# A decoder block in split fp32: activation sums moved between unit pairs, w_down's fourth operand summed by DMA, and the first up units interleaved

## The chip, the cores and the metric

The kernel runs on one core of one Trainium2 chip. The metric is device time of one execution, in microseconds (us), the median over runs. TensorE (PE) multiplies, VectorE (DVE), ScalarE (ACT) and GpSimd (POOL) work on the operands, and SyncE (SP), POOL and ACT issue the DMAs. "PEld" is TensorE's loading of weights, which runs beside its matmuls.

## What is computed

One residual decoder layer on x of 512 positions by 1024 channels, all in float32. The change touches the second half, the channel sub-layer:

```python
h2 = rms_norm(x, norm2_g) * (1 + scale2) + shift2
u = causal_dwconv(h2 @ w_up, conv_w, conv_b)      # w_up: 1024 x 5632, window 3
u_g, u_v = jnp.split(u, 2, axis=-1)               # 2816 channels each
x = x + gate2 * ((jax.nn.silu(u_g) * u_v) @ w_down)
```

The vectors shift, scale and gate come from c through `ada_w`, 6 groups of 1024 columns; group 5 is gate2. The first half (attention with block selection, a pooling mixer, their gated sum and w_out) is not touched.

## The kernel before

**Split operands.** Every float32 operand of a matmul is split in two: a high half `hi` (ACT copies it to the fp32r type) and a low half `lo = raw - hi` (DVE). A product is then three matmuls: hi times hi, hi times lo, lo times hi (`mm3`, L127; `more`, L133, the same as a continuation of an open sum). `up_mm` (L1140) runs `mm3` over the 8 row blocks k of a unit, where a unit is 128 of w_up's columns. Matmuls take 512 positions, or 256 where only one half of the positions is ready or where the seven-product scheme works on halves.

**Order.** PE, DVE and ACT run in the order in which the program names the instructions; SP's and POOL's DMAs are placed by a planner at build time and issue as soon as what they wait for is done. Buffers are rings or pools of fixed size: `wraw` 5 raw weight units (128 x 1024), `whi` and `wlo` 4 each, `slots` 68 tiles of 128 x 512, 8 PSUM banks.

**First up units (L1328 to L1338).** When w_out's last products end, the first half of the positions is already normalized and transposed (`h2h`, `h2l`, by `take_h2(1, ...)`); the second half is still going through `o_norm` (L1042: the tiles `xn`). Units 0 to 3 start on positions 0 to 255. Unit 0 takes hi and lo weights times h2h for all k first and h2l after that (`up_late`, L1132). After unit 1 come the transposes of the second half (`turn_h2(3)`, PE line L919), `take_h2(3)`, which makes h2h and h2l of it block by block (ACT L932 and L934, DVE L935), and two ada sums; then units 2 and 3, and last all four units on positions 256 to 511. `ahead(name, n)` (L112) prepares the hi and lo halves (ACT L109, DVE L119) up to n units past the named one; up to six units are prepared this way.

**The up loop (L1423).** Pair j (0 to 21) is the gate unit and the value unit of 128 channels. Pairs in `SEVEN` (5, 6, 8, 9, 10, 12, 13, 14, 16 to 19) are computed with seven products of half size in place of eight (Strassen's scheme, Winograd's form; `seven`, L1291), 84 matmuls of 256 positions each; they need sums of the two weight units (`prep_seven`, L1248: steps s0 to s3, with halves named G, t1, R and V), made while the pair before is multiplied. R's second half is added in DVE line L1279. The other pairs are plain: 48 matmuls of 512 positions. In `seven`, `keep` (L1305) lets ACT copy a PSUM sum aside before the sum goes on; `ka` and `kb` are such copies.

**Behind the matmuls.** One pair late, `behind(0)` runs the convolution of pair j - 1 (`glu_a`; ACT L1124, four DVE steps L1128) and `behind(1)` its silu and product (`glu_b`; DVE L1158). Four pairs make one unit i of w_down's input (`fa["a11", i]` and so on; unit i has the pairs 4i to 4i + 3, and there are NU = 6 units, the last one half as wide). When the pair listed in `S_AT` has been through `behind(1)`, `s_sum` (L1164, DVE L1167) forms s1 = a21 - a22 of the unit with that place in the list, and the next `behind(0)` runs `s_split` (L1169): hi and lo of s1 and a11 (ACT L1176, DVE L1179) and the sums s2 and s3 (DVE L1181, L1182). `s_forms` is both at once. In a plain pair `behind(0)` comes after all preparation steps but the last, in a pair of seven products after the second (after the first where the next pair is plain).

**The down phases (L1515).** `w_down` is multiplied in seven products too, one after the other over all six units, 66 matmuls of 512 columns per phase (in the last one, two units are cut in halves). Here they are numbered 1 to 7: a11 b11, s1 t1, s2 t2, a12 b21, s3 t3, s4 b22, a22 t4. `d_ahead` keeps the splits of the weight operands (`d_split`; ACT L1391, DVE L1393) two units ahead. t1, t2 and t4 are running sums: the tile `ta` holds b11, and after its split an accumulating DMA from POOL's queue (L1396) adds b12, which makes t1, and after that b22, which makes t2. t4 is t2 + b21: `d_load` loads b21 again as a raw unit, and `d_add` (L1372, DVE L1378) adds `ta`. Around the matmuls of a unit the program places the splits of the activations for later phases (`split_s`, `split_a`; L214 and L215), the sum s4 (L1546), and the ada sums (`ada_col`: a load of 128 x 1024 into `wraw` and one DVE operation, L202). `finish` (L1476) combines the kept sums, multiplies by gate2, adds the residual and stores; it needs gate2 as rows, which `row_out` (L834, a small DMA of POOL) and `row_in` (ACT's queue) turn round.

Of the kernel before, what the change touches and what calls it, by code (L numbers as in the profile page):

```python
# [10 lines left out]
ALU = mybir.AluOpType  # L11
# [8 lines left out]
KT = D // P  # L20
# [14 lines left out]
PLAIN = 3  # L35
# [20 lines left out]
def block_kernel(tc, x, cvec, ada, wtok, wch, pool_w, wbr, wout, wup, wdn, pack, table, out):  # L56
# [4 lines left out]
    with ctx:  # L61
# [18 lines left out]
        def load_unit(src, name):  # L80
            raw = wraw_p.tile([P, src.shape[-1]], F32, tag="raw", name=f"raw_{name}")
            nc.sync.dma_start(raw, src)
            return raw
# [1045 lines left out]
                        t[:, n:], ps[:, : S - n], cw(i, 2 - n), t[:, n:], op0=ALU.mult, op1=ALU.add)  # L1129
            return res  # L1130

        def up_late(ps, w, c0, c1):  # L1132

            for k in range(KT):
                nc.tensor.matmul(ps[:, c0:c1], w[0][:, tslice(k)], h2h[k][:, c0:c1], start=k == 0, stop=False)
                nc.tensor.matmul(ps[:, c0:c1], w[1][:, tslice(k)], h2h[k][:, c0:c1], start=False, stop=False)
            for k in range(KT):
                nc.tensor.matmul(ps[:, c0:c1], w[0][:, tslice(k)], h2l[k][:, c0:c1], start=False, stop=k == KT - 1)

        def up_mm(ps, w, c0, c1):  # L1140
            for k in range(KT):
# [185 lines left out]

        first = []  # L1328
        for i in range(4):
            ahead(f"up{i}", min(2, 2 * PLAIN - 1 - i))  # L1330
            first.append((ready.pop(f"up{i}"), bank(f"u_{i}")))
            (up_mm if i else up_late)(first[i][1], first[i][0], 0, 256)
            if i == 1:
                take_h2(3, turn_h2(3))
                ada_col(5, 0)
                ada_col(5, 1)
        for w, ps in first:
            up_mm(ps, w, 256, 512)  # L1338
        pend, summed = [], []
        S_AT = [4, 7, 19, 20]  # L1340

        tsum = {("t3", i): dpool.tile([P, width(i)], F32, name=f"tsum_t3_{i}") for i in range(NU)}

# [14 lines left out]
        def d_load(m):  # L1358

            n, i = divmod(m, NU)  # L1360
            nm, w = FORMS[n], width(i)
            src = lambda b, c0=0, c1=w: wdn[plain[b], i][:, c0:c1]
            if nm == "b11":
                ta[i] = [slot(f"ta_{i}_{u}") for u in range(w // 512)]
                for u, t in enumerate(ta[i]):
                    nc.sync.dma_start(t, src("b11", u * 512, u * 512 + 512))
            elif nm[0] == "b" or nm == "t4":
                draw[m] = load_unit(src("b21" if nm == "t4" else nm), f"{nm}_{i}")
            elif nm == "t3":
                draw[m] = load_unit(tsum["t3", i], f"t3_{i}")  # L1370

        def d_add(m):  # L1372

            i = m - 6 * NU
            if 0 <= i < NU:
                for u, t in enumerate(ta.pop(i)):
                    r = draw[m][:, u * 512 : u * 512 + 512]
                    nc.vector.tensor_add(r, r, t)  # L1378

        def d_split(m):  # L1380

# [17 lines left out]
        def d_ahead(m):  # L1399

            m = min(m, len(FORMS) * NU - 1)
            while done[1] <= m:
                while done[0] <= min(done[1] + 2, len(FORMS) * NU - 1):
                    d_load(done[0])
                    done[0] += 1
                d_split(done[1])
                done[1] += 1
                d_add(done[1])

        def behind(n):  # L1410

# [11 lines left out]
        for j in range(NP):  # L1423
            if j + 1 == NP:
                steps = [lambda: d_ahead(0), lambda: d_ahead(1)]
            else:
                steps = [] if j < PLAIN else (prep_seven if j + 1 in SEVEN else prep_two)(j + 1)
            if j < 2:
                u = first[2 * j][1], first[2 * j + 1][1]
                behind(0)  # L1430
                if j == 1:
                    for st in prep_two(PLAIN):
                        st()
                behind(1)
                h_forms(j)
                ada_col(5, 2 + j)
            elif j in SEVEN:
                if len(steps) == 2:
                    mine = [steps[:1], [lambda: behind(0)], [lambda: behind(1)], steps[1:]]
                else:  # L1440
                    mine = [steps[:1], steps[1:2] + [lambda: behind(0)], steps[2:3] + [lambda: behind(1)], steps[3:]]
                u = seven(j, lambda n: [f() for f in mine[n]])
            else:
                if j < PLAIN:
                    for e in range(2):
                        upw[j, e] = ready.pop(f"up{2 * j + e}")
                u = [bank(f"u_{2 * j + e}") for e in range(2)]
                for st in steps[:-1]:
                    st()
                up_mm(u[0], upw.pop((j, 0)), 0, S)  # L1450
                behind(0)
                for st in steps[-1:]:
                    st()
                up_mm(u[1], upw.pop((j, 1)), 0, S)
                behind(1)
                if j in (2, 3):
                    h_forms(j)
            pend.append((j, *u))
            sum_load(j + 3)
            if j % 2 == 0:  # L1460
                t3_sum(j // 2)
        s_forms(NU - 2)
        behind(0)
        behind(1)

# [49 lines left out]
        for n, (an, bn, acc) in enumerate(phases):  # L1515
            last = n == len(phases) - 1
            held_ = []
            for i in range(NU):
                d_ahead(n * NU + i + (3 if n == i == 0 else 2))
                w = dready.pop(n * NU + i)  # L1520
                if due:
                    due.pop(0)()
                a = forms.pop((an, i))
                if last and i >= NU - 2:
                    held_.append((a, w, width(i) // 512))
                else:
                    for u in range(width(i) // 512):
                        for p in range(2):
                            step(acc, p, u, a, w, 0, 512, i == NU - 1 and u == width(i) // 512 - 1)
                if n == 0:  # L1530
                    if i == 2:
                        s_forms(NU - 1)
                    if i > 1:
                        split_s(i - 2)
                    if i == NU - 1:
                        ada_col(5, 4)
                elif n == 1:
                    if i in (0, 2, 4):
                        ada_col(5, 5 + i // 2)
                    if i < 2:  # L1540
                        split_s(NU - 2 + i)
                    forms["a12", i] = split_act(fa["a12", i], f"a12_{i}", width(i) // 2)
                elif n == 2:
                    split_a("s3", i)
                    s2 = fa.pop(("s2", i))
                    nc.vector.tensor_add(s2, s2, fa.pop(("a12", i)))  # L1546
                    fa["s4", i] = s2
                elif n == 3:
                    split_a("s4", i)
                    split_a("a22", i)  # L1550
                    if i == 2:
                        g2 = row_in(g2d, "g2", nc.scalar)
            if last:
# [6 lines left out]
                keep("s1", "X")  # L1560
            elif n == 1:
                keep("s5", "Y")
                g2d = row_out(5, "g2")
            elif n == 2:
                keep("s2", "X")
                fetch(0, 0)
# [78 lines left out]
```

## Time and profile before

| | |
|---|---|
| median of 3 runs | 669.06 us (667.11 to 671.19) |
| the profiled execution | 667.67 us, its span (first to last instruction) 665.9 us |
| mean granted TensorE clock | 0.997 |
| DMA | 140.21 MB, mean 211 GB/s |
| DMAs of `ta` from w_down, POOL's queue | 22 of 256 KB, median 8.8 us from issue to landing |
| loads of `raw_ada`, SP's queue | 48 of 512 KB, median 5.1 us |

Times in the views are counted from the first instruction. A row of the timeline gives start, length, engine, line, operation, written tile <- read tiles, shape, count, and in brackets how long the engine sat idle before it and what ended that. A row of the stretches gives the stretch, its length, then busy time and instructions of PE, PEld, DVE, ACT and POOL, the granted clock, the DMA engines' busy share and GB/s. A row of the waits gives the waiting instruction, what it waited for, the sum, the number of times and the longest. Matmul lengths overlap, since they are pipelined: how fast PE goes is read from starts or from a stretch and its count. PE's stretches used below are: first units 311.25 to 337.55, pairs 2 to 21 from there to 550.94, phase 1 from 550.94, phase 2 from 567.62, phase 4 from 597.54, phase 7 from 643.25.

### The profile page before, as it was taken

Reading aid. Unit: us, or ns where it says so; the run is one execution under the profiler, and the core shown is the slowest. Engines: PE = TensorE matmul, PEld = TensorE weight load, DVE = VectorE, ACT = ScalarE, POOL = GpSimd, SP = SyncE. Lnnn points to the kernel's source line nnn. Section 1 sums busy time; section 2 is a strip of 40 time slices with the busy share of each in tenths; the row PEclk is TensorE's granted clock in tenths of the full one; section 3 lists DMA queues with packets and bytes.
Section 4 is the critical chain, followed back from the end, with each engine's and each line's share of the span. In section 5 each row is a group of like instructions: output and inputs, shape, how many; then the busy total and the mean of one; then the engine's idle time right before and its main releaser. Section 6 shows DMA issues by size and latency. Waiting matters only on the chain.

```text
span 665.9 us, 10016 instructions
## 1 busy us (share of the span) xinstructions
PE 649.7 (98%) x3541; PEld 561.9 (84%) x3541; DVE 571.2 (86%) x990; ACT 394.6 (59%) x716; POOL 159.0 (24%) x203
## 2 busy tenths in 40 slices
PE   7999999999999999999999999899999999999996
PEld 5788788888888888888988999889999987878884
DVE  6997888898878878999699898978879989989776
ACT  7655346756665566576655666556657746768421
POOL 3003154433200046513411212121222023500000
PEclk9999999999999999999999999899999999999999
DMA  8887248999852686467877577584868485957841
GB/s 342 303 301 284 69 173 264 273 274 316 258 180 96 224 181 228 179 220 249 226 248 190 159 203 200 163 232 114 228 174 239 155 240 121 233 121 243 282 171 64
DMA packets 47657, 140.21 MB, mean 211 GB/s; under 512 B 6019, under 2 KB 6700, under 8 KB 47606
## 3 DMA queue, kind: packets, MB, share of 16 engines
q1 hardware_dynamic: 30230, 98.76, 43.2%
q0 software_dynamic: 17088, 40.28, 26.0%
q10 hardware_dynamic: 288, 0.52, 0.3%
q8 instruction: 28, 0.46, 0.3%
q14 instruction: 23, 0.19, 0.1%
HBM read 128.24 MB, written 11.30 MB: 210 GB/s over the span
## 4 chain that ended last, share of the span: by engine, by line
PE 72%; DVE 15%; DMA 5%; ACT 4%; issue 3%; SPq 1%; POOL 0%; ACTq 0%; DVEq 0%
PE gate_ps L128 4%; PE gate_ps L129 4%; PE gate_ps L130 4%; PE u L129 4%; PE u L130 4%; PE u L128 4%; DMA ta<-in_wdn 3%; PE uX L134 2%; PE uX L136 2%; PE uX L135 2%; PE q L144 2%; PE p L144 2%; DVE lo_t L1393 2%; PE O L641 2%; DVE uv L1128 1%
## 5 line engine op out<-in xcount | busy, mean ns | idle before, releaser
L128 PE MATMUL u<-h2h,hi_up 128*128 128x512 f32 (+1 forms) x184 | 65.8, 358 | 0.0
L129 PE MATMUL u<-h2l,hi_up 128*128 128x512 f32 (+1 forms) x184 | 65.7, 357 | 0.0
L130 PE MATMUL u<-h2h,lo_up 128*128 128x512 f32 (+1 forms) x184 | 65.6, 357 | 0.0
L202 DVE CUSTOM_DVE_ANT_0 raw_ada<-raw_ada,cbc,pk 128x1024 f32<-128x1024 f32 x48 | 60.8, 1278 | 0.2 <-DMA raw_ada<-in_ada 0.2
L128 PE MATMUL gate_ps<-h_h,hi_gate 128*128 128x512 f32 x128 | 50.1, 391 | 0.0
L130 PE MATMUL gate_ps<-h_h,lo_gate 128*128 128x512 f32 x128 | 50.0, 390 | 0.0
L129 PE MATMUL gate_ps<-h_l,hi_gate 128*128 128x512 f32 x128 | 50.0, 390 | 0.0
L130 PEld LDWEIGHTS u<-h2h,lo_up 128*128 128x128 f32 x184 | 34.8, 189 | 5.0
L128 PEld LDWEIGHTS u<-h2h,hi_up 128*128 128x128 f32 x184 | 34.8, 189 | 4.9
L129 PEld LDWEIGHTS u<-h2l,hi_up 128*128 128x128 f32 x184 | 34.8, 189 | 4.8
L1255 ACT ACTIVATE hi_upR<-raw_up 128x512 fp32r<-128x512 f32 x24 | 15.1, 629 | 26.8 <-DVE raw_up L1279 18.9
L1396 POOL DMA_DIRECT2D ta<-in_wdn x22 | 18.9, 1105 | 45.3 <-DVE lo_b L1393 39.9
L130 PEld LDWEIGHTS gate_ps<-h_h,lo_gate 128*128 128x128 f32 x128 | 24.0, 188 | 5.1
L128 PEld LDWEIGHTS gate_ps<-h_h,hi_gate 128*128 128x128 f32 x128 | 24.0, 188 | 4.9 <-DVE mn L600 0.3
L604 ACT ACTIVATE L<-L,mn 128x512 f32<-128x512 f32 (+3 forms) x32 | 17.6, 552 | 17.3 <-DVE mn L600 17.3
L129 PEld LDWEIGHTS gate_ps<-h_l,hi_gate 128*128 128x128 f32 x128 | 24.0, 188 | 4.5
L119 DVE TENSOR_TENSOR lo_gate<-raw_gate,hi_gate 128x1024 fp32r<-128x1024 f32 x16 | 19.5, 1221 | 6.6 <-ACT hi_gate L109 6.6
L1391 ACT ACTIVATE hi_t<-raw_t 128x1024 fp32r<-128x1024 f32 (+1 forms) x12 | 11.9, 990 | 22.2 <-DVE raw_t L1378 14.5
L109 ACT ACTIVATE hi_up<-raw_up 128x1024 fp32r<-128x1024 f32 x20 | 20.8, 1050 | 4.3 <-PE u L129 4.3
L1260 DVE TENSOR_TENSOR lo_upG<-raw_up,hi_upG 128x1024 fp32r<-128x1024 f32 x12 | 14.7, 1222 | 9.7 <-ACT hi_upG L1255 9.7
L1260 DVE TENSOR_TENSOR lo_upR<-raw_up,hi_upR 128x1024 fp32r<-128x1024 f32 x12 | 14.7, 1226 | 8.4 <-ACT hi_upR L1255 8.4
L1246 POOL DMA_DIRECT2D ur<-in_wup x12 | 10.4, 897 | 42.4 <-DMA ur<-in_wup 25.6
(426 smaller groups left out, 2311.6 us busy)
## 6 DMA issues: line engine op xcount, KB each, us to landing
raw_ada<-in_ada SPq DMA_DIRECT2D x48, 512.0 KB, 5.1
raw_up<-in_wup SPq DMA_DIRECT2D x44, 512.0 KB, 4.6
raw_gate<-in_wch SPq DMA_DIRECT2D x16, 512.0 KB, 5.2
tc<-in_wdn POOLq DMA_DIRECT2D x22, 256.0 KB, 3.5
ta<-in_wdn POOLq DMA_DIRECT2D x22, 256.0 KB, 8.8
raw_b<-in_wdn SPq DMA_DIRECT2D x10, 512.0 KB, 6.2
ta<-in_wout POOLq DMA_DIRECT2D x16, 256.0 KB, 7.6
raw_br<-in_wbr SPq DMA_DIRECT2D x8, 512.0 KB, 4.4
```

What stands on the lines that cost most here:

```text
L109: nc.scalar.activation(hi, raw, AF.Copy)
L119: nc.vector.tensor_sub(lo, raw, hi.bitcast(F32))
L128: nc.tensor.matmul(ps, sh, mh, start=start, stop=False)
L129: nc.tensor.matmul(ps, sh, ml, start=False, stop=False)
L130: nc.tensor.matmul(ps, sl, mh, start=False, stop=stop)
L134: nc.tensor.matmul(ps, sh, mh, start=start, stop=False, skip_group_check=True)
L144: nc.tensor.matmul(ps, sl if i else sh, mh if i else ml, start=False, stop=stop and i != late)
L202: nc.vector.tensor_tensor_reduce(out=raw, in0=raw, in1=cbc, op0=ALU.mult, op1=ALU.add, scale=1.0, scalar=col(C_AB + i), accum_out=acol[:, ...
L604: nc.scalar.activation(L[:, :n], L[:, :n], AF.Exp, scale=-1.0, bias=mn, accum_out=sm)
L1255: nc.scalar.activation(hi[:, c], raw[:, c], AF.Copy)
L1260: nc.vector.tensor_sub(lo, raw, hi.bitcast(F32))
L1396: nc.gpsimd.dma_start(t, wdn[plain[NEXT[nm]], i][:, cs], accum_op=ALU.add)
```

## The change

It has four parts.

1. **First units.** `up_both` multiplies units 0 and 1 together, block k of both before block k + 1; for the first positions with h2l last, for the second with h2l in its place. The transposes of the second half come after unit 2 instead of unit 1. Units 4 and 5 are prepared after the interleaved second halves, instead of during units 2 and 3.
2. **Activation sums.** `S_AT` becomes 5, 9, 17, 19: units 0 to 3 are summed in pairs 6, 10, 18, 20 and split in pairs 7, 11, 19, 21 (before: summed in 5, 8, 20 and 21, split in 6, 9, 21 and after the loop). Units 4 and 5 are formed in phase 1, after its second and third unit (before: after the loop, and after the third unit). The ada sums 4 to 7 of gate2 go from phases 1 and 2 into pairs 7, 11, 15 and 20, and `row_out` to phase 1.
3. **Splits of the down phases** are spread: s2 over phases 1 and 2 later than before, s3 over phases 3 and 4, a22 over phases 5 and 6 (before: s3 in phase 3, a22 in phase 4).
4. **t4.** b21 is added to `ta` by two accumulating DMAs per unit from POOL's queue; each follows a one-column DVE copy of the tile onto itself, placed in phase 5 after the matmuls of unit i. The raw loads of b21 for t4 and the DVE additions are gone.

```diff
-        def up_late(ps, w, c0, c1):
...
+        def up_both(units, c0, c1, late):
+            n = len(units)
             for k in range(KT):
+                for w, ps in units:
+                    nc.tensor.matmul(ps[:, c0:c1], w[0][:, tslice(k)], h2h[k][:, c0:c1], start=k == 0, stop=False,
+                                     skip_group_check=True)
+                    nc.tensor.matmul(ps[:, c0:c1], w[1][:, tslice(k)], h2h[k][:, c0:c1], start=False, stop=False,
+                                     skip_group_check=True)
+                    if not late:
+                        nc.tensor.matmul(ps[:, c0:c1], w[0][:, tslice(k)], h2l[k][:, c0:c1], start=False,
+                                         stop=k == KT - 1, skip_group_check=True)
+            for w, ps in units if late else ():
+                for k in range(KT):
+                    nc.tensor.matmul(ps[:, c0:c1], w[0][:, tslice(k)], h2l[k][:, c0:c1], start=False,
+                                     stop=k == KT - 1, skip_group_check=True)
...
         for i in range(4):
-            ahead(f"up{i}", min(2, 2 * PLAIN - 1 - i))
+            ahead(f"up{i}", min(2, 3 - i))
             first.append((ready.pop(f"up{i}"), bank(f"u_{i}")))
-            (up_mm if i else up_late)(first[i][1], first[i][0], 0, 256)
             if i == 1:
+                up_both(first, 0, 256, True)
+            elif i > 1:
+                up_mm(first[i][1], first[i][0], 0, 256)
+            if i == 2:
                 take_h2(3, turn_h2(3))
                 ada_col(5, 0)
                 ada_col(5, 1)
-        for w, ps in first:
+        up_both(first[:2], 256, 512, False)
+        ahead("up5", 0)
+        for w, ps in first[2:]:
             up_mm(ps, w, 256, 512)
...
-        S_AT = [4, 7, 19, 20]
+        S_AT = [5, 9, 17, 19]
...
-            elif nm[0] == "b" or nm == "t4":
-                draw[m] = load_unit(src("b21" if nm == "t4" else nm), f"{nm}_{i}")
+            elif nm[0] == "b":
+                draw[m] = load_unit(src(nm), f"{nm}_{i}")
...
-        def d_add(m):
-            i = m - 6 * NU
-            if 0 <= i < NU:
-                for u, t in enumerate(ta.pop(i)):
-                    r = draw[m][:, u * 512 : u * 512 + 512]
-                    nc.vector.tensor_add(r, r, t)
+        def d_four(i):
+            for u, t in enumerate(ta[i]):
+                nc.vector.tensor_copy(t[:, :1], t[:, :1])
+                nc.gpsimd.dma_start(t, wdn[plain["b21"], i][:, u * 512 : u * 512 + 512], accum_op=ALU.add)
...
                 done[1] += 1
-                d_add(done[1])
...
+                if j in (7, 11, 15, 20):
+                    ada_col(5, {7: 4, 11: 5, 15: 6, 20: 7}[j])
...
-        s_forms(NU - 2)
         behind(0)
         behind(1)
...
                 if n == 0:
-                    if i == 2:
-                        s_forms(NU - 1)
-                    if i > 1:
-                        split_s(i - 2)
-                    if i == NU - 1:
-                        ada_col(5, 4)
+                    if i in (1, 2):
+                        s_forms(NU - 3 + i)
+                    if i > 3:
+                        split_s(i - 4)
+                    if i == 1:
+                        g2d = row_out(5, "g2")
                 elif n == 1:
-                    if i in (0, 2, 4):
-                        ada_col(5, 5 + i // 2)
-                    if i < 2:
-                        split_s(NU - 2 + i)
+                    if i < 4:
+                        split_s(2 + i)
...
                 elif n == 2:
-                    split_a("s3", i)
+                    if i < 3:
+                        split_a("s3", i)
...
+                elif n in (4, 5):
+                    if n == 4:
+                        d_four(i)
+                    if i % 2 == n % 2:
+                        split_a("a22", i)
                 elif n == 3:
+                    if i < 3:
+                        split_a("s3", 3 + i)
                     split_a("s4", i)
-                    split_a("a22", i)
...
             elif n == 1:
                 keep("s5", "Y")
-                g2d = row_out(5, "g2")
```

More of the change, by code (lines that the diff above doesn't have):

```diff
@@ L1130, in convs @@
             return res
-        def up_late(ps, w, c0, c1):
+        def up_both(units, c0, c1, late):
+            n = len(units)
             for k in range(KT):
[L1135 to L1138, printed above, removed]
+                for w, ps in units:
[10 more added lines that the diff above has]
+                                     stop=k == KT - 1, skip_group_check=True)
         def up_mm(ps, w, c0, c1):
```

## The prediction, made before the changed kernel ran

> **What bounds the kernel now.** First the page's busy times and the chain that ended last, then the waits of TensorE (PE), then the stretches in which they lie.
>
> ```profile
> PE 649.7 (98%) x3541; PEld 561.9 (84%) x3541; DVE 571.2 (86%) x990; ACT 394.6 (59%) x716; POOL 159.0 (24%) x203
> PE 72%; DVE 15%; DMA 5%; ACT 4%; issue 3%; SPq 1%; POOL 0%; ACTq 0%; DVEq 0%
> ```
> ```profile
> PE uX L134 <- ACT ka L1305: 3.0, 1, 3.0
> PE X L135 <- DVE lo_b L1393: 1.4, 1, 1.4
> ```
> ```profile
> 311.25:337.55 26.30, 25.43 (x210) 24.86 (x208) 20.49 (x39) 17.30 (x34) 9.38 (x15) 1.00 0.77 229
> 411.35:421.43 10.08, 10.08 (x87) 10.08 (x85) 9.60 (x15) 7.94 (x17) 1.59 (x4) 1.00 0.68 206
> 421.43:436.23 14.80, 11.82 (x87) 11.61 (x85) 12.89 (x23) 7.59 (x14) 3.88 (x5) 0.88 0.62 178
> 550.94:567.62 16.68, 15.26 (x67) 12.31 (x66) 16.20 (x31) 11.47 (x22) 7.57 (x9) 1.00 0.60 116
> 567.62:582.58 14.96, 14.96 (x67) 12.39 (x66) 14.96 (x26) 11.00 (x22) 7.91 (x10) 1.00 1.10 240
> 597.54:613.33 15.79, 15.26 (x68) 12.31 (x66) 15.79 (x22) 14.27 (x23) 0.00 (x0) 1.00 0.69 231
> 643.25:662.20 18.95, 16.43 (x85) 13.29 (x83) 15.51 (x25) 3.81 (x4) 0.00 (x0) 1.00 0.12 42
> ```
> PE is full; the change neither adds nor removes a matmul, so only PE's lost time can move. The rows (length, then PE, weight loads, DVE, ACT, POOL, clock, DMA) give it by stage against clean ones. A clean sevens pair is 84 matmuls of 256 columns in 10.08 us, 0.120 each; a clean phase is 66 of 512 columns in 14.96, 0.227 each. Hence: the first units (192 x 0.120 and 16 transposes, 1.8 by the row of 15 below, 24.8) lose 1.5; pair 10 loses 4.7 (14.80 - 10.08); phase 1 loses 1.7; phase 4 loses 0.8; phase 7 (48 x 0.227 + 36 x 0.120 + 0.2 = 15.4) loses 3.6. In all 12.3 us, and that is the most the change can win.
>
> **First units, +1.4 us.**
> ```profile
> 313.48 0.38 PE L1135 MATMUL u<-h2h,hi_up 128*128 128x256 f32 x1 [0.40 <-ACT h2h L934]
> 315.88 2.00 ACT L109 ACTIVATE hi_up<-raw_up 128x1024 fp32r<-128x1024 f32 x2
> 317.25 1.68 DVE L1045 TENSOR_SCALAR xn<-x,rs_y 128x512 f32<-128x512 f32 x4 [0.48 <-POOL rs_y L1040]
> 318.58 1.86 PE L919 MATMUL hT<-pk,xn 128*128 128x128 f32 x15 [0.40 <-DVE xn L1045]
> 318.84 2.35 DVE L119 TENSOR_TENSOR lo_up<-raw_up,hi_up 128x1024 fp32r<-128x1024 f32 x2
> 326.55 0.43 DVE L935 TENSOR_TENSOR h2l<-h2f,h2h 128x256 fp32r<-128x256 f32 x1 [0.48 <-ACT h2h L934]
> ```
> Now unit 0 outruns h2h (the 0.40 row) and the transposes of the second half wait for xn. Interleaving doubles a block's work to 4 x 0.12, so the first wait goes; the transposes come after unit 2, so the second goes: -1.5. But unit 2 now stands where they stood. Units 0 and 1 end at 311.25 + 48 x 0.12 = 317.0; unit 2's third matmul, due at 317.25, reads its low half, which DVE makes in program order behind the four xn: 318.84 + 1.22 = 320.06 (half of the 2.35). PE waits 2.8 us, with the restart 2.9. Behind it nothing waits: transposes from 322.7, the last h2l 8 us later (now from 318.58 to 327), while unit 3 and the interleaved second halves (0.72 a block) reach the last block at 332.3. Net -1.5 + 2.9 = +1.4. Ends: -1.5 if the low half were early, +2.9 if the clock also drops. up4 and up5 are prepared only after the interleaved halves end at 333.1: by 2.00 / 2 and 2.35 / 2 a unit their lows are there by 336.6, and pair 2 begins at 338.9, so 0.
>
> On the drop: the wait of 3.0 us in pair 10 cost 4.7, 1.7 more than itself, with a granted clock of 0.88 in that row. A wait of 2.8 may or may not do the same: 0 to 1.5 us, and I take 0. The Trainium skill (TensorE: Matmul & The Clock Gate, "What's actually happening") lets the clock fall after an idle window of about 3.4 us; by it neither wait would cost more than itself. The row disagrees for 3.0.
>
> **Pairs 5 to 19, -3.5 us.**
> ```profile
> 421.21 0.68 DVE L1179 TENSOR_TENSOR s_l<-s,s_h 128x512 fp32r<-128x512 f32 x1
> 423.95 0.68 DVE L1279 TENSOR_TENSOR raw_up<-raw_up 128x512 f32<-128x512 f32 x1
> 424.67 0.63 ACT L1255 ACTIVATE hi_upR<-raw_up 128x512 fp32r<-128x512 f32 x1 [4.66 <-DVE raw_up L1279]
> 427.03 0.37 ACT L1305 ACTIVATE ka<-uX 128x256 f32<-128x256 f32 x1
> ```
> This chain is pair 10's loss: s_split in pair 9 (four DVE steps from 421.21 on, and one small product before L1279's 423.95: 2.4 us for the four) delays L1279, ACT waits for it with hi_upR, and ka, which frees X, is queued behind on ACT. From the add's end (424.63) to ka's end (427.40) it takes 2.8; X is wanted 24 x 0.12 = 2.9 into the pair. So the add has to end by 0.1 after its own pair's end. Pair 9's is 3.1 late.
>
> The new places: unit 0 is summed in pair 6 and split in 7, unit 1 in 10 and 11, unit 2 in 18 and 19. 7 and 11 are plain, and also get an ada sum.
> ```profile
> 390.85 1.14 ACT L1255 ACTIVATE hi_upG<-raw_up 128x512 fp32r<-128x512 f32 x2
> 393.91 1.22 DVE L1260 TENSOR_TENSOR lo_upG<-raw_up,hi_upG 128x1024 fp32r<-128x1024 f32 x1
> 404.36 1.23 DVE L1260 TENSOR_TENSOR lo_upG<-raw_up,hi_upG 128x1024 fp32r<-128x1024 f32 x1 [0.93 <-ACT hi_upG L1255]
> 406.72 0.69 DVE L215 TENSOR_TENSOR ut_l<-ur,ut_h 128x512 fp32r<-128x512 f32 x1 [0.41 <-ACT ut_h L214]
> 410.38 0.68 DVE L1279 TENSOR_TENSOR raw_up<-raw_up 128x512 f32<-128x512 f32 x1
> 413.69 0.69 DVE L1167 TENSOR_TENSOR s<-a,a 128x512 f32<-128x512 f32 x1
> 450.22 1.23 DVE L1260 TENSOR_TENSOR lo_upG<-raw_up,hi_upG 128x1024 fp32r<-128x1024 f32 x1 [2.80 <-ACT hi_upG L1255]
> 466.67 0.69 DVE L1279 TENSOR_TENSOR raw_up<-raw_up 128x512 f32<-128x512 f32 x1
> 523.46 8.84 SPq L82 DMA_DIRECT2D raw_ada<-in_ada  x4
> 326.89 1.28 DVE L202 CUSTOM_DVE_ANT_0 raw_ada<-raw_ada,cbc,pk 128x1024 f32<-128x1024 f32 x1
> ```
> Pair 7 gains 2.4 + 1.3 = 3.7 us of DVE. Pair 6 gives its split away, so DVE enters pair 7 earlier, by 1.9 at most (393.91 against ACT's 391.99). The idle 0.93 and 0.41 take most of the other 1.8: 0.4 late. Pair 8's add, 411.06 now and due at 411.45, is just in time. Pair 9 loses its split (2.4) and pair 8's sum (0.6), so its add goes from 424.63 to 422.0, still 0.5 late: I charge 0.7 with restarts. 4.7 becomes 0.7: -4.0. Ends: -4.7, and -2.1 if DVE gets no lead into pair 7.
> Pair 11 likewise gains 3.7, against 2.80 and 0.41: 0.5 late, and pair 13's add (467.36, pair end 467.29) has no room: +0.5 (0 to 1.0). Pairs 14, 18 and 19 prepare less or have their add done; pairs 15 and 20 hide one ada. Each ada's load also stands on SP's queue and takes one of five raw buffers: I take 0, with the fourth rival's price as the other end.
>
> **Phases 1 and 4, -2.4 us.**
> ```profile
> 551.20 0.78 ACT L1124 ACTIVATE uv<-u,pk 128x512 f32<-128x512 f32 x1 [0.71 <-PE u L130]
> 557.45 3.70 DVE L1393 TENSOR_TENSOR lo_b<-ta,hi_b 128x512 fp32r<-128x512 f32 x6
> 579.69 0.84 POOL L1396 DMA_DIRECT2D ta<-in_wdn  x1 [1.17 <-DVE lo_t L1393]
> 594.71 0.63 ACT L1391 ACTIVATE hi_t<-ta 128x512 fp32r<-128x512 f32 x1 [3.00 <-DMA ta<-in_wdn]
> ```
> Phase 1's third unit waits for lo_b, at 557.45 behind three splits. Two leave the stretch, 4.8 us; the last convolution can then start at 552.0 and, with three more of its steps and two products, lets lo_b start at 554.7, 1.7 before PE wants it. Unit 4's split now runs inside phase 1, done by 560.8, and its operands are due at 561.8: a spare of 0.2 to 2, so -1.6 and not -1.7. Phases 1 and 2 lose four ada sums, 5.1 us of DVE, so ta's last accumulation is issued some 2.7 us earlier against phase 1's start, while PE comes 1.7 earlier; phase 3's tail also drops an s3 split (0.6). The 0.8 goes. row_out's DMA moves on POOL's queue ahead of the accumulations of units 4 and 5: one more issue (0.84) before transfers that are wanted 10 us later, 0. Ends: 0 and -2.5.
>
> **Phase 7, -3.5 us.**
> ```profile
> L1396 POOL DMA_DIRECT2D ta<-in_wdn x18: 841/1040/2322, 558.7 to 579.7; - x18
> 558.66 5.21 POOL L1396 DMA_DIRECT2D ta<-in_wdn  x6 [10.50 <-DVE lo_b L1393]
> 617.50 1.22 DVE L1393 TENSOR_TENSOR lo_t<-raw_t,hi_t 128x1024 fp32r<-128x1024 f32 x1
> 636.34 1.29 DVE L1378 TENSOR_TENSOR raw_t<-raw_t,ta 128x512 f32<-128x512 f32 x2
> 638.88 1.23 DVE L1393 TENSOR_TENSOR lo_t<-raw_t,hi_t 128x1024 fp32r<-128x1024 f32 x1 [1.26 <-ACT hi_t L1391]
> ```
> Today each t4 unit costs DVE 1.2 for the add, 1.26 of waiting for ACT and 1.2 for the low half: 3.7, against PE's 12 x 0.227 = 2.7. The adds become DMAs. Left are 1.3 a unit and 4 us of finishing: DVE fits, and the loss goes. The DMAs start behind a one-column copy in phase 5, near 617.5, two per 2.7 us; POOL issues one in 0.87 (5.21 / 6), and the slow landing above took 15 us (579.69 to 594.71). The last, issued near 630, lands by 645; PE takes that unit from 654 (643.25 + 4 x 2.72). Hidden, with 7 us to spare after a split. The copies (a 128x1 operation; I take 0.1, at most 0.4 like the smallest step of 256 columns) wait for nothing still running, and DVE's queue goes on behind them; the moved s3, s4 and a22 splits fit as well: phases 3 to 6 hold at most 14 us of DVE in 15.
>
> **Sum.** +1.4 - 4.0 + 0.5 - 2.4 - 3.5 = -8.0 us. The profiled execution took 667.67 (span 665.9), so 659.7; it is 1.4 below the median 669.06 of three runs, and against that median the forecast is 661.0.
>
> **Rivals.**
> 1. Unit 2's low half is ready in time, if xn and it run sooner than I read: -10.9, 658.2. Against it: DVE is in program order, and the chain before xn is not touched.
> 2. t4's DMAs come late, since POOL builds them while DVE is busy. If each issue took the longest in its row, 2.3 us, eleven take 25; the last is issued at 643, lands at 658, and PE waits 5 us: 666. Against it: the 0.87, taken beside a busy DVE, and a median of 1.04. The Trainium skill has such a rule (SBUF — State Buffer, "A bandwidth-pool intuition that's wrong"): a POOL-issued DMA takes some 3.1 us beside a DVE copy instead of 0.62. By it the last issue would be at 652. The trace bears out a third of that at the median.
> 3. DVE gets no lead into pairs 7 and 11, and the half clock follows unit 2's wait: +1.9 + 0.5 + 1.5, 664.9.
> 4. Slower: each ada holds a raw buffer, so the next V half loads, accumulates and is added late; the sevens after pairs 7, 11 and 15 wait. At 4.7 a place, as pair 10 shows, 14.1 less 8.0: 675. It turns the result from 2.7 a place on. Against it: now four sums are loaded at once, from 523.46 on, and no pair after that waits.
> 5. The sums do not fall into plain pairs as said: three are formed in sevens and unit 2 is split in one, pair 19. If that costs its 0.6 and 2.4 in full: 664.
>
> **How the numbers follow.** Forecast 661.0: 0.55. Rivals: 0.09, 0.11, 0.13, 0.05, 0.07. From 656 (nearly the full 12.3, on either base) to 666 (rivals 2 and 3) little but the fourth is left out. A measurement here tells about 0.5%, 3.3 us: faster means under 665.7. Forecast and rivals 1, 3 and 5 are faster, 0.84; rival 2 is mostly no change, 0.11; slower 0.05.
>
> **What would show it.** PE waits about 2.8 us on lo_up (L119) at the third unit and not on xn or h2h; pair 10 takes 10.1 to 10.8 us at a clock of 1.00; phases 1, 4 and 7 take about 15 us; no ACT hi_t of phase 7 waits for DMA ta. A pair between 8 and 19 over 12 us, or a wait on ta in phase 7, would make the prediction wrong.

## The result and the profile after

The changed kernel takes 663.14 us (median of 8 runs, 661.28 to 665.26) against 667.77 us of the kernel before on the same chip (8 runs, 664.43 to 671.19): a ratio of 0.9925, 95% interval 0.9897 to 0.9953. The forecast was 661.0 (656 to 666). The direction and most of the steps hold; one step has the wrong sign.

The page of the changed kernel: PE is busy for nearly the same time, and the chain that ended last has more of PE in it and less of DVE (82 and 9% against 72 and 15%).

```profile
PE 648.4 (98%) x3541; PEld 560.8 (85%) x3541; DVE 564.0 (85%) x995; ACT 395.3 (60%) x721; POOL 167.2 (25%) x214
PE 82%; DVE 9%; DMA 4%; ACT 2%; issue 2%; SPq 1%; POOL 0%; DVEq 0%; ACTq 0%
```

The stretches of the changed kernel, in the columns of the prediction (length, PE, PEld, DVE, ACT, POOL, clock, DMA share, GB/s): first units, pair 10, phase 1, phase 4, phase 7 with the tail.

```profile
309.99:337.72 27.73, 25.10 (x210) 24.88 (x209) 19.68 (x38) 16.29 (x33) 10.07 (x16) 1.00 0.68 193
421.60:431.91 10.31, 10.31 (x86) 10.12 (x85) 9.48 (x17) 7.71 (x14) 2.93 (x4) 1.00 0.68 207
546.76:565.98 19.22, 16.17 (x68) 12.15 (x66) 13.40 (x25) 9.82 (x19) 6.11 (x8) 1.00 0.92 164
595.90:610.86 14.96, 14.96 (x67) 12.39 (x66) 11.40 (x16) 11.62 (x19) 0.00 (x0) 1.00 0.67 226
640.78:660.27 19.49, 15.36 (x85) 13.28 (x83) 11.18 (x21) 2.94 (x5) 0.00 (x0) 0.97 0.19 66
```

Against before: first units +1.43, pair 10 -4.49, pair 14 +0.13, phase 1 +2.54, phase 4 -0.83, phase 7 with the tail -3.16 (22.65 before; the clock of 0.97 in its row falls behind the last matmul). The stretch ahead of the first units, where nothing is changed, was 1.26 shorter in this execution (309.99 against 311.25; in the other kernels below it lies between 309.90 and 311.47, with no pattern). The other stages are within 0.02, and the sum is the difference of the spans, 665.9 - 660.3 = 5.6 us.

What PE waits for in the whole of the changed kernel, its three longest sums that lie behind the start:

```profile
PE u L130 <- DVE lo_up L119: 2.6, 1, 2.6
PE X L135 <- DVE lo_b L1405: 2.2, 3, 1.6
PE X L134 <- ACT hi_b L1403: 0.9, 1, 0.9
```

The first is unit 2's low half. The other two are phase 1. Before, PE waited there once, 1.4 us for lo_b in the third unit. Now hi_b is late in the fifth unit (0.9), and lo_b behind it (1.6 of the 2.2). There the question lies.

### The profile page after: what moved, and what is told of

Read it like the earlier page. It is cut to its first block, busy times and chain, and to the rows that moved or that the text cites. A ratio compares the mean times of both kernels' runs of the same rounds, so it can differ in the third digit from the quotient of the medians.

```text
span 660.3 us, 10023 instructions
## 1 busy us (share of the span) xinstructions
PE 648.4 (98%) x3541; PEld 560.8 (85%) x3541; DVE 564.0 (85%) x995; ACT 395.3 (60%) x721; POOL 167.2 (25%) x214
## 4 chain that ended last, share of the span: by engine, by line
PE 82%; DVE 9%; DMA 4%; ACT 2%; issue 2%; SPq 1%; POOL 0%; DVEq 0%; ACTq 0%
PE gate_ps L128 4%; PE gate_ps L130 4%; PE gate_ps L129 4%; PE u L130 4%; PE u L128 4%; PE u L129 4%; DMA ta<-in_wdn 3%; PE uX L134 3%; PE uX L136 2%; PE uX L135 2%; PE X L135 2%; PE X L136 2%; PE X L134 2%; PE q L144 2%; PE p L144 2%
## 5 line engine op out<-in xcount | busy, mean ns | idle before, releaser
L130 PE MATMUL u<-h2h,lo_up 128*128 128x512 f32 (+1 forms) x160 | 58.9, 368 | 2.6 <-DVE lo_up L119 2.6
L128 PE MATMUL u<-h2h,hi_up 128*128 128x512 f32 (+1 forms) x160 | 59.1, 369 | 0.0
L129 PE MATMUL u<-h2l,hi_up 128*128 128x512 f32 (+1 forms) x160 | 58.9, 368 | 0.0
L130 PEld LDWEIGHTS u<-h2h,lo_up 128*128 128x128 f32 x160 | 30.2, 188 | 7.9 <-DVE lo_up L119 2.8
L128 PEld LDWEIGHTS u<-h2h,hi_up 128*128 128x128 f32 x160 | 30.2, 189 | 4.9
L129 PEld LDWEIGHTS u<-h2l,hi_up 128*128 128x128 f32 x160 | 30.2, 189 | 4.7
L1405 DVE TENSOR_TENSOR lo_t<-ta,hi_t 128x512 fp32r<-128x512 f32 x33 | 21.3, 688 | 4.2 <-ACT hi_t L1403 4.2
L1403 ACT ACTIVATE hi_t<-ta 128x512 fp32r<-128x512 f32 x33 | 19.1, 623 | 7.4 <-PE Y L136 4.1
L837 POOL DMA_DIRECT2D g_d<-acol x2 | 1.8, 923 | 72.9 <-DVE acol L202 48.4
```

The lines of the kernel that those rows point to most:

```text
L128: nc.tensor.matmul(ps, sh, mh, start=start, stop=False)
L129: nc.tensor.matmul(ps, sh, ml, start=False, stop=False)
L130: nc.tensor.matmul(ps, sl, mh, start=False, stop=stop)
L1403: nc.scalar.activation(hi[:, cs], t, AF.Copy)
L1405: nc.vector.tensor_sub(lo[:, cs], t, hi[:, cs].bitcast(F32))
```

## The experiments

**What phase 1 waits for.** In phase 1 the first split that is late is ACT's, and it waits for data:

```profile
ACT hi_b L1403 <- DMA ta<-in_wdn: 4.2, 3, 2.5
```

The same execution's timeline has the two issues in question, the small DMA of gate2 on POOL's queue (`row_out`, 4 KB, 1024 elements of four bytes, each to an address of its own) and, within 0.12 us, the first of ta's last five loads on SP's. Ahead of both stands DVE's last step of the last ada sum, in pair 20:

```profile
536.15 0.08 DVE L202 DVE_READ_ACCUMULATOR2_ANT acol<- 128x1 f32 x1
536.53 0.93 POOL L837 DMA_DIRECT2D g_d<-acol  x1 [24.42 <-DMA ta<-in_wdn]
536.65 6.82 SPq L1380 DMA_DIRECT2D ta<-in_wdn  x5
```

The small DMA writes out what the ada sums leave in `acol`, and it is issued 0.3 us after the last of them. Before, that sum stood in phase 2, and the DMA went out at 582.71, behind phase 2.

The DMA view of the changed kernel between 534 and 566 us. The first two rows are the DMA engines' busy share (tenths) and GB/s in 40 slices of 0.8 us; an issue row ends with the median time from issue to landing.

```profile
DMA  8999999999999978875965999999999999407979
GB/s 225 338 374 341 366 387 394 407 400 329 218 74 44 38 59 100 125 64 72 95 36 92 233 307 277 261 241 230 220 210 207 213 202 207 72 15 84 205 92 187
...
ta<-in_wdn SPq DMA_DIRECT2D x5, 256.0 KB, 17.5
...
g_d<-acol POOLq DMA_DIRECT2D x1, 4.0 KB, 13.0
```

From 542.8 to 551.6 us (slices 12 to 22) the engines are five to nine tenths busy and yet move 36 to 125 GB/s, about a fifth of what they moved just before. In the kernel before, ta's loads of these 32 us landed after 5.9 us:

```profile
ta<-in_wdn SPq DMA_DIRECT2D x8, 256.0 KB, 5.9
```

**Theory A**: the small DMA makes everything beside it slow. **Theory B**: the loads of b21 do it. The ada sums used to hold the raw buffers at this point; now the buffers are free, and the planner puts five loads of b21 (512 KB each, issued 25.7 to 10.5 us ahead of phase 1, where before had one) on SP's queue ahead of ta's last loads.

**The kernel again**, unaltered.

> The changed kernel once more, unaltered. Phase 1 took 19.2 us in the first profile (a clean phase: 14.96). If that loss is chance of one execution, phase 1 is under 16 us here; if it belongs to the kernel (either to row_out's small DMA in phase 1, or to b21's raw loads standing ahead of ta's last loads on SP's queue), it is 18 to 20 us again. The first units' wait on unit 2's low half (2.6 us in the first profile) should be there in any case, with or without a half-clock window behind it.

Measured: 661.33 us (7 runs, 659.55 to 665.5), ratio 0.9912 (0.9881 to 0.9943); phase 1 18.24 us. The loss belongs to the kernel, though not its exact size.

**row_out back in the program** at the end of phase 2.

```diff
-                    if i == 1:
-                        g2d = row_out(5, "g2")
...
                 keep("s5", "Y")
+                g2d = row_out(5, "g2")
```

> The changed kernel with row_out alone moved back from phase 1 to the end of phase 2. Theory A (its 1024 four-byte writes clog the DMA engines while ta is loaded): phase 1 falls from 19.2 to 15 to 16 us, and the time by about 3.5 us against the changed kernel. Theory B (b21's raw loads ahead of ta's last loads on SP's queue): phase 1 stays at 18 to 20 us, time unchanged.

Measured: 661.44 us (4 runs), ratio 0.9898 (0.9874 to 0.9922); phase 1 17.02 us. This does not tell the theories apart, since the small DMA was issued 10.2 us ahead of phase 1 all the same, 0.3 us after the last ada sum:

```profile
537.57 0.08 DVE L202 DVE_READ_ACCUMULATOR2_ANT acol<- 128x1 f32 x1
537.95 0.92 POOL L837 DMA_DIRECT2D g_d<-acol  x1 [24.42 <-DMA ta<-in_wdn]
```

So it was the ada sum's move to pair 20 that brought the DMA forward, and not the move of its line: a DMA of the planner's goes out when its data are there.

**The small DMA held** behind phase 2, by something it must wait for.

```diff
-                    if i == 1:
-                        g2d = row_out(5, "g2")
...
                 keep("s5", "Y")
+                nc.vector.tensor_copy(acol[:, 47:48], acol[:, 47:48])
+                g2d = row_out(5, "g2")
```

> The change whole, but the small DMA that writes gate2 as a row (row_out, 1024 writes of four bytes) is held until the end of phase 2, where it stood before, by a one-column copy of its source on VectorE. The order of the loads on SP's queue up to phase 1 is the same as in the changed kernel: only the small DMA moves. Theory A (the small DMA slows every other packet for some 9 us, so ta's loads for units 3 to 5 land 11 to 15 us into phase 1): the spell from -4 to +4 us around phase 1 goes, ta's last loads land before +4, phase 1 takes 15.0 to 15.6 us instead of 18.2 to 19.2, the span falls by 3 to 4 us to about 656.5. Theory B (the loads of b21, hoisted ahead of ta's last loads on SP's queue, delay them): phase 1 stays at 17 to 19 us and the time at 661 to 663.

Measured: 660.93 us (4 runs), ratio 0.9887 (0.9852 to 0.9922). The small DMA was issued at 578.52. Phase 1 in the stretches of this kernel, and the DMA view of the same 32 us (phase 1 begins at 548.23 here):

```profile
548.23:563.75 15.52, 15.24 (x67) 12.31 (x66) 13.22 (x25) 9.50 (x19) 6.20 (x8) 1.00 0.80 137
```
```profile
DMA  7977999999999999999995000098999999999999
GB/s 266 364 248 264 318 364 402 420 407 415 394 379 230 223 225 266 369 389 287 205 187 97 10 0 0 0 172 159 120 136 166 184 205 169 136 164 156 174 169 156
...
ta<-in_wdn SPq DMA_DIRECT2D x7, 256.0 KB, 5.3
```

The loads of b21 stand where they stood, the dip is gone, ta lands after 5.3 us instead of 17.5, and phase 1 is 3.7 us shorter than in the first profile of the changed kernel (2.7 than in the second). Theory B alone, which expected 17 to 19, is out. The span fell by 2.3 only (658.0), since in this execution the first units took 29.26 us, a part of them at half clock; more on that below.

**The loads of b21 held** instead, the small DMA left where it is.

```diff
-                draw[m] = load_unit(src(nm), f"{nm}_{i}")
+                raw = wraw_p.tile([P, w], F32, tag="raw", name=f"raw_{nm}_{i}")
+                if nm == "b21":
+                    nc.vector.tensor_copy(raw[:, :1], col(0))
+                nc.sync.dma_start(raw, src(nm))
+                draw[m] = raw
```

> The change whole, with the small DMA of gate2 where the change has it, 10 us ahead of phase 1; but each load of b21 for phase 4 follows a one-column VectorE write of its buffer, placed where the program loads it, so that none stands ahead of ta's loads on SP's queue. Theory A: the slow spell is still there (packets of 2048 bytes at 300 ns and more for 8 us), part of ta's loads still lands in it or behind it; since 1 MB less goes through the spell, phase 1 comes down a little, to 16.5 to 18 us. Theory B: ta's last loads are issued and land ahead of phase 1 and it takes 15.0 to 15.6 us, with the spell of slow packets gone as well or harmless. In both, the later loads of b21 may cost phase 4 up to 1 us.

Measured: 660.39 us (4 runs), ratio 0.9875 (0.9837 to 0.9912). Phase 1, and the summary of the DMA view of 542 to 550 us:

```profile
549.22:564.75 15.53, 15.26 (x68) 12.31 (x67) 13.22 (x25) 9.50 (x19) 6.17 (x8) 1.00 1.02 206
```
```profile
DMA packets 50, 0.10 MB, mean 13 GB/s; under 512 B 0, under 2 KB 0, under 8 KB 50
```

Here theory A's 16.5 to 18 misses too. Without the b21 loads in front, the planner issues ta's loads for units 0 to 3 from 25.3 us ahead of phase 1 on, and they are in before the small write begins; what is left in its spell is not wanted in a hurry. So the loss needs both: a spell of some 9 us in which little moves, and loads pushed into it that phase 1 is about to want. Either one taken away ends it. Its size is not fixed: in the seven profiles here that have both, phase 1 takes 16.49 to 19.22 us, so the loss against the 15.52 is 1.0 to 3.7.

**The first part undone**: first units as before, all else as changed.

> The changed kernel with the first up units as before (unit 0 alone, transposes after unit 1, units 4 and 5 prepared early). If the working of the prediction holds, the first units take 26.3 us in place of 27.6, so 1.3 us less than the changed kernel, and up to 1.7 more where the changed kernel's wait also costs half-clock time. If instead interleaving as such gains, it is slower than the changed kernel.

Measured: 659.17 us (4 runs, 658.61 to 659.77), ratio 0.9866 (0.9842 to 0.989); first units and phase 1:

```profile
310.39:336.69 26.30, 25.43 (x209) 24.86 (x208) 20.48 (x39) 17.28 (x34) 9.33 (x15) 1.00 0.75 225
545.73:562.54 16.81, 15.60 (x68) 12.24 (x66) 13.34 (x25) 9.63 (x19) 6.17 (x8) 1.00 1.01 193
```

The first part costs 1.43 us at full clock. In the timed runs it seems to cost more: the mean clock of all four runs here is 0.998 to 1.000, while in the changed kernel's eight it is 0.997 or less in seven. (One window of 3.41 us at half clock lowers the mean by 0.003; three of the eight are at 0.994 or less, and where they lose the rest no profile shows. Phase 1 is shorter here too, so the medians do not give the first part alone.) The held-row kernel shows where a window goes. Its first units have the same wait of 2.6 us, and this clock:

```profile
309.90:339.16 29.26, 26.63 (x210) 26.38 (x208) 19.70 (x38) 16.31 (x33) 11.15 (x17) 0.94 0.69 195
```

**Unit 2's low half first**, the remedy that the prediction's first units suggest: its hi and lo halves are made before the squares of the norm and before xn.

```diff
+        early["up2"] = load_unit(plan[pos["up2"]][0], "up2")
+        his["up2"] = hi_of("up2", early["up2"])
         for p in range(2):
             o_square(2 + p, 1, True)
...
+        ahead("up2", 0)
```

> The changed kernel with unit 2's high half made on ACT ahead of the squares and its low half on DVE ahead of the normalization xn. If the wait of 2.6 us is only DVE's order, it shrinks to under 0.7 us and the first units take 25 to 25.7 us, 2 us less than the changed kernel. If xn moved later by about 0.4 to 0.8 us is on the path, the transposes wait instead and nothing is won.

Measured: 659.83 us (4 runs), ratio 0.9875 (0.985 to 0.99). First units, then pair 5 and pair 13:

```profile
309.98:335.56 25.58, 25.04 (x210) 24.84 (x209) 19.67 (x38) 16.28 (x33) 10.46 (x15) 1.00 0.64 175
368.22:379.90 11.68, 10.34 (x86) 10.13 (x85) 11.52 (x17) 7.83 (x16) 1.46 (x2) 1.00 0.64 181
452.51:463.88 11.37, 10.33 (x87) 10.13 (x86) 10.04 (x16) 7.48 (x16) 1.48 (x3) 1.00 0.77 193
```

The wait shrinks to 0.5 and the first units gain 2.15, but pairs 5 and 13 lose 1.6 and 1.3 to waits for ka, which the changed kernel doesn't have. POOL's last accumulation of a weight half goes out 4.5 us ahead of pair 5 there (at 363.74 us), against 8.3 in the changed kernel; that this is the cause was not tried.

**t4's additions back on DVE** (`d_add` and the raw loads of b21 in place of `d_four`).

> The change whole, but t4's part undone: b21 is loaded again as a raw unit and VectorE adds ta to it, two units ahead in phase 7, as before; no accumulating DMA in phase 5. If phase 7's gain comes from the adds alone: phase 7 with the tail goes from 19.5 back to 22.6 us, phases 2 to 6 stay within 0.3 us, the span is 3.2 us longer than the changed kernel's, 663 to 664, and the time no longer differs from the kernel before by more than 0.5%. Rival: the splits taken out of the late phases made the room, and phase 7 stays under 20.5 us.

Measured: 665.51 us (10 runs), ratio 0.9967 (0.9937 to 0.9996); phase 7 with the tail:

```profile
641.83:666.54 24.71, 17.91 (x85) 14.74 (x83) 17.27 (x27) 4.02 (x5) 0.00 (x0) 0.93 0.12 43
```

PE waits 2.5 us for lo_t and 0.5 for hi_t again, the longest of these waits 1.45, and the clock halves for 3.4 us. Phases 2 to 6 do not move. Phase 7's gain is that of the additions; the rival, room made by the moved splits, is out.

**The old list of pairs**, `S_AT = [4, 7, 19, 20]`.

> The change whole, but the list of the pairs after which the activation sums are formed is again 4, 7, 19, 20; the ada sums stay in pairs 7, 11, 15 and 20. If the split of unit 1 in pair 9 is what made pair 10 wait: pair 10 goes from 10.3 back to about 14.8 us (a wait of 3 us, and half clock behind it), pair 14 returns from 10.3 to 10.2, the span is 4 to 5 us longer than the changed kernel's, 664 to 665. Rival: the ada sums and not the splits decide where DVE is late, and pair 10 stays under 11.5 us.

Measured: 667.87 us (10 runs, 664.82 to 670.06), ratio 1.0003 (0.9979 to 1.0026). Pair 10, and PE's wait in it:

```profile
422.25:435.55 13.30, 10.33 (x86) 10.13 (x85) 12.46 (x23) 7.70 (x14) 2.37 (x3) 1.00 0.43 89
```
```profile
PE uX L134 <- ACT ka L1314: 3.0, 1, 3.0
```

The same 3.0 us for ka, and DVE's instructions are 23 again instead of 17. Pair 10 is 13.30 and not 14.80, since the clock held in this execution. The split in pair 9 makes the loss, and not the ada sums, which stand here as in the change. Without this part the whole change is worth nothing that these runs can tell.

**Both losses out**: first units as before, small DMA held.

> The change whole, with its first part (the interleaved first units) undone and gate2's small DMA held until the end of phase 2. If the two are independent: first units 26.3 us, with no wait over 1 us and so no half clock there; phase 1 at 15.5 us; all other stages as in the changed kernel; span 659.2 - 1.3 = 655.5 to 656 us and a median near 657.5, 0.984 to 0.986 of the kernel before. Rival: a later stage gives part of it back, or phase 1 takes 16 us and more, since ta's loads stand at other times against it.

Measured: 656.90 us (5 runs, 656.71 to 657.24), ratio 0.9836 (0.981 to 0.9861). First units, pair 10, phase 1, phase 7:

```profile
309.98:336.30 26.32, 25.45 (x210) 24.87 (x209) 20.49 (x39) 17.30 (x34) 9.35 (x15) 1.00 0.75 222
420.18:430.49 10.31, 10.31 (x87) 10.13 (x85) 9.46 (x17) 7.71 (x14) 2.57 (x4) 1.00 0.79 212
545.32:560.84 15.52, 15.25 (x68) 12.31 (x67) 13.22 (x25) 9.50 (x19) 6.20 (x8) 1.00 0.80 137
635.64:655.12 19.48, 15.35 (x85) 13.28 (x83) 11.17 (x21) 2.94 (x5) 0.00 (x0) 0.97 0.18 65
```

In the profiles the two add up (660.3 - 1.41 - 3.70 = 655.2, measured 655.1), and this version beats both kernels. In the timed runs the first part weighs more and the small DMA less: with the DMA held, undoing the first part takes the ratio from 0.9887 to 0.9836, some 3.4 us; with the first part undone, holding the DMA takes it from 0.9866 to 0.9836, some 2.0. The intervals of each two overlap a little, so these sizes are rough.

**The interleaving alone**, with the transposes after unit 1 (`if i == 2` becomes `if i == 1`) and the small DMA held.

> The change whole, with gate2's small DMA held until the end of phase 2 and, of the first part, only the interleaving of units 0 and 1 kept: the transposes of the second half stay after unit 1, as before. If the first part's loss comes from the move of the transposes alone: PE waits 0.5 to 0.7 us for xn again and not 2.6 for the low half of unit 2, the first wait of 0.4 for h2h is gone, and the first units take 25.7 us, 0.6 less than with the whole part undone and 2 to 3.5 less than in the changed kernel; the median is 0 to 0.6 us under that of the kernel with the first part undone, near 657. Rival: the interleaving itself costs, or the later preparation of units 4 and 5 does, and the first units take 26.5 us and more or pair 2 waits.

Measured: 657.00 us (6 runs), ratio 0.9837 (0.9811 to 0.9863); first units 26.30 us, no gain over the 26.30 to 26.32 of the old order. PE's wait there:

```profile
PE hT L919 <- DVE xn L1045: 1.1, 2, 0.7
```

The wait of 0.4 for h2h goes, and the wait for xn grows from 0.4 to 1.1: the transposes start when xn is there, whatever PE does before. The expectation of 25.7 missed that. Pair 13 also takes 10.72 us instead of 10.08; why is left open.

**Fewer, larger packets.** Two kernels turn gate2 by one transpose of TensorE, copy it to 8 rows and write 8 packets of 512 bytes. The first does it behind the last pair, in the changed kernel.

```diff
+        def row_flat(g, name):
+            gd = dpool.tile([1, D], F32, name=f"{name}_d")
+            tp = bank(f"{name}_T")
+            nc.tensor.transpose(tp[:8, :P], acol[:, 8 * g : 8 * g + 8], ident)
+            fl = slot(f"{name}_f")
+            nc.scalar.activation(fl[:8, :P], tp[:8, :P], AF.Copy)
+            nc.gpsimd.dma_start(gd.rearrange("o (k p) -> (o k) p", p=P), fl[:8, :P])
+            return gd
...
+        g2d = row_flat(5, "g2")
...
-                    if i == 1:
-                        g2d = row_out(5, "g2")
```

> The change whole, but gate2 is turned by TensorE (one transpose of 128 x 8) behind the last pair, copied by ScalarE to 8 rows of 128, and written by 8 packets of 512 bytes instead of 1024 of 4 bytes, at about the start of phase 1, in the midst of ta's loads. The transpose and its copy cost up to 0.5 us of the path. Theory A, if it is the four-byte writes that slow the others: no spell of slow packets after it, phase 1 at 15.0 to 16 us. Theory B: phase 1 stays at 17 to 19 us, since the loads of b21 stand where they stood.

Measured: 660.93 us (4 runs), ratio 0.989 (0.9849 to 0.9931); phase 1 16.47 us, 0.47 above the expectation; ACT's first split of phase 1 starts 0.9 us later than with the row held (3.94 us into the phase against 3.05). It doesn't settle what it was made for: the write went out at 549.24, when ta's loads had all but landed, so there was hardly anything for it to slow. And 16.47 is hardly less than the 16.49 of the kernel with unit 2's low half first, which has the element-wise write.

The second does it between the two units of the last pair, with the first units as before, so that the write goes out while loads are under way.

> The change with its first part undone, and gate2 turned by TensorE (one transpose of 128 x 8) between the two units of the last pair, copied to 8 rows of 128 and written by 8 packets of 512 bytes, about 5 us ahead of phase 1, while ta's last loads are under way. To be read against the same kernel with the 1024 four-byte writes 10 us ahead of phase 1 (phase 1 16.8 us) and with them held behind phase 2 (15.5 us). Theory: it is the many four-byte packets that hold up the loads beside them. Then 8 packets hold up nothing: the small write lands in under 5 us, packets of 2048 bytes stay under 200 ns in the mean, ta's last loads land before +4, phase 1 takes 15.4 to 15.8 us, the span is 655 to 655.8 and the median 656.5 to 657.5. Rival: any small write to memory in the midst of the loads does it, whatever its packets: phase 1 takes 16.3 us or more.

Measured: 657.19 us (4 runs), ratio 0.984 (0.9799 to 0.9881). Phase 1, and the DMA view of 534 to 566 us (phase 1 begins at 546.96):

```profile
546.96:562.51 15.55, 15.25 (x67) 12.32 (x66) 13.22 (x25) 9.50 (x19) 6.21 (x8) 1.00 0.76 127
```
```profile
GB/s 225 348 353 410 374 428 405 420 374 361 259 230 220 237 373 382 289 200 189 133 15 0 0 0 54 187 136 123 154 156 154 166 169 151 154 174 192 133 156 141
...
g_d<-g_f POOLq DMA_DIRECT2D x1, 4.0 KB, 4.5
```

The same 4 KB in 8 packets land after 4.5 us in the midst of loads at 220 to 382 GB/s, and nothing dips. With the 1024 small elements (the kernel with the first part undone) phase 1 takes 16.81 us; with these 15.55, as if the DMA were not there. Beside the form of the write, its time of issue differs (4.7 us ahead of phase 1 against 10.2), which no run takes apart. That the form counts is borne out by the element-wise write's 8.4 us with little beside it, almost twice these 4.5 beside loads.

## Why the prediction was right, and where it was not

**First units, +1.4: right.** PE waits 2.6 us for lo_up (2.9 with the restart foretold) and the stretch grows by 1.43. The half clock behind it, which I took as 0 out of 0 to 1.5, comes in half of the profiles with this wait (four of eight, all four from one chip, though mean clocks of 0.992 in timed runs on another show drops there too) and costs 1.5 there, so in the timed runs the part costs more than its 1.4.

**Pairs 5 to 19, -3.5: right, and a little low.** Pair 10 gains 4.49 (-4.0), since DVE is not late for pair 9's add at all; pairs 11 to 14 lose 0.13 (+0.5). The old list alone brings the 3.0 us back. The other end, that an ada sum's raw buffer delays a V half, did not come.

**Phases 1 and 4, -2.4: this step failed.** Phase 4's -0.8 came (-0.83), and since phase 4 also takes 14.96 us with the small DMA back behind phase 2, that DMA's absence is not the reason. Phase 1 was to gain 1.6 and lost 2.54, which is 4.1 of error in one term. The reasoning on DVE was nearly sound: with the small DMA held, phase 1 takes 15.52, a gain of 1.16 of the 1.6, and PE waits there once, for 0.3 us. What failed is the sentence on row_out's DMA: "one more issue (0.84) before transfers that are wanted 10 us later, 0". The place was wrong: I took the DMA to go out in phase 1, where its line stands, and it went out 10.2 us ahead of phase 1, when the last ada sum was done. The price was wrong too: I priced the DMA by its issue on POOL and not by what it does to the DMA engines, though it stood in the trace of before: there it was 13.2 us from issue to landing for 4 KB. The landing of ta that the prediction calls slow (14.9 us) has that write issued 3.0 us behind it; without it, the last of ta lands after 8.0 us in the changed kernel. And I moved the ada sums out of phases 1 and 2 without asking what the planner would do with the buffers they free. My ends for this step, 0 and -2.5, did not hold the result, since I bounded it by DVE and PE alone.

**Phase 7, -3.5: right** (-3.16). t4's DMAs hide, no ACT hi_t waits for them, and a one-column copy costs the 0.1 us that I took:

```profile
617.91 0.21 DVE L1389 COPY ta<-ta 128x1 f32<-128x1 f32 x2
```

**The sum**: -8.0 foretold, -4.4 measured in the changed stages of the profiled execution, -4.6 in the medians. The error is phase 1's 4.1, and phase 7's 0.3, less 0.9 that the pairs gained above their term. That the time still lies between 656 and 666 is in part luck: the range was made wide for other rivals (2 and 3), none of them a loss in phase 1. Of the signs that the prediction names, a phase 1 of about 15 us is the one that did not come.

**The rivals.** Unit 2's low half was not early (1), t4's DMAs not late (2), DVE had its lead (against 3, of which only the half clock behind unit 2's wait came, at times), and sums in sevens cost nothing that shows (5). The fourth, held raw buffers, was the nearest and the wrong way round: one half of the harm came from buffers being free too early.

## What to carry to other kernels

Price a DMA by its packets and by what shares the engines with it, not by its issue: a transfer of a few KB in single elements wants a place where nothing urgent is in flight, or a turn through TensorE first. Where a planner places the DMAs, ask of every buffer that an edit frees which load will now go early, and ahead of what; and hold a DMA by data that it must wait for, since its line in the program does not. When parts of a change are measured together, undo each once: here two parts carried the gain, and two others gave more than half of it back (663.1 us against the 656.9 without their losses).

## What the runs showed of the hardware

The small write takes 8.4 us from issue to landing where it is held behind phase 2, with only the last accumulations of ta ahead of it, 10.2 where b21's loads are held, and 11.5 to 13.2 beside them. The DMA engines' rate in the 8 us of the spell, and in the corresponding 8 us ahead of phase 1 without it (changed kernel from 542, held row from 543.5):

```profile
DMA packets 381, 0.71 MB, mean 89 GB/s; under 512 B 42, under 2 KB 42, under 8 KB 381
```
```profile
DMA packets 1106, 2.01 MB, mean 251 GB/s; under 512 B 126, under 2 KB 126, under 8 KB 1106
```

The write of gate1's row has the same spell in both kernels, near 235 us (from 234 to 242 the changed kernel moves 63 GB/s, from 226 to 234 it moves 263). The Trainium skill (DMA: Bandwidth & Descriptors, "Why small descriptors are slow (HBM only)") has small packets paying a fixed overhead each, which speaks of the write's own time. The 8.4 us for 4 KB are of that kind, but no run here shows that this overhead makes them up; that the packets beside it wait too is what these traces add. Where in the engines or the memory they wait is not shown.

A wait of 2.63 us on PE was followed by 3.41 us at half clock in four profiles (as in the 0.94 row above) and not in four others with the same wait to within 10 ns; the waits of 0.4 to 0.7 alone never were. In phase 7 with t4's additions back, 3.41 us at half clock come behind waits of 1.45, 0.48 and 0.34 us that lie close together. The Trainium skill (TensorE: Matmul & The Clock Gate, "What's actually happening") puts the idle window at about 3.4 us; these runs have the drop after shorter waits, sometimes, so the measurement decides: a wait of 2.6 us, or a group of shorter ones such as these, is to be priced with and without the 1.5 us.
